# Products of a weight piece reordered: part, k tile, output tile in place of output tile, k tile, part

## The chip, the core and the metric

The kernel runs on one NeuronCore of a Trainium2 chip. TensorE (PE) multiplies, VectorE (DVE) and ScalarE (ACT) do everything elementwise, GpSimd (POOL) and SyncE (SP) issue transfers. The metric is the device time of one execution in microseconds, median of the runs.

## What is computed

Two layers of a decoder trunk for a prompt of 256 tokens and a sample group of 8 x 4 tokens, with shared weights. Layer 0 mixes tokens by causal pooling, layer 1 by multi-scale retention. The reference, cut to what matters here:

```python
for i in range(DEPTH):
    h = _rmsnorm(x, norm_mix[i])
    y = pool_mixer(h) if i % 2 == 0 else retention(h, ret_w_in, ret_w_out)
    x = x + y
    h = _rmsnorm(x, norm_ffn[i])
    u = einsum('btd,df->btf', h, w_up)          # 2048 -> 11264
    c = causal_conv3(u); gate, up = split(c)
    x = x + einsum('btf,fd->btd', silu(gate) * up, w_down)   # 5632 -> 2048
    gate = sigmoid(einsum('btd,de->bte', _rmsnorm(x, norm_ple[i]), ple_w_gate[i]))
    x = x + gate * einsum('btp,pd->btd', p[i], ple_w_proj[i])
return _rmsnorm(x, norm_final), new states
```

All in float32. D_MODEL is 2048, FFN_DIM 5632, PLE_DIM 256, 8 heads.

## The kernel before

Tokens lie on the free axis: 256 of the prompt and 32 of the sample make one moving operand of 288 columns. Weights are the stationary operand, 128 x 128 at a time. A float32 product is made of three products of the type fp32r: both the weights and the activations are split into a high and a low part, and hi·hi, hi·lo and lo·hi are added up in PSUM (the function `three`, lines 265 to 267; in the trace `xh,hi`, `xl,hi`, `xh,lo`, activations first).

The weights come in **pieces** of 256 x 512: two k tiles (`kk`) of 128 rows, four output tiles (`m`) of 128 columns. A piece is loaded into `raw`, ScalarE casts it to `hi` (L1402), VectorE subtracts to get `lo` (L1410). A piece takes 24 products: 4 output tiles x 2 k tiles x 3 parts. There are 864 pieces, and 20,736 such products.

Pieces belong to **groups**: one group makes four output tiles and runs over all its K rows, `K // 2` pieces. The 168 groups are, in order: pooling (4 groups of 2 pieces), per FFN 22 up groups of 8 pieces and 24 down groups of 2 or 4, per embedding 4 gate groups of 8 pieces and 4 groups `emb` of one piece, and in the retention 8 groups each for q and k (A), v (B) and the gate (C), of 8 pieces, and 32 output groups (O) of 2.

Each output tile of a group adds up in a PSUM bank of its own, taken from a ring of five (`pbank`, name `mm`). When the last piece of a group is through with output tile m, `g.evac` is issued at once: it reads the bank on VectorE (lines 604 and 605 for an up group, 722 for down, 1361 for O, 1001 for C, 859 for emb, 532 for pooling) or ScalarE (958 for A, 993 with 994 on VectorE for B). The bank is free for the next group when that is done. A group needs four banks and the ring has five, so its first tile gets the bank that was left over, and tiles 1, 2 and 3 get those of tiles 0, 1 and 2 of the group before.

What is issued around the products is set by a program at build time: after each of the four quarters of a piece (6 products, a "tick") it issues operations of other work on the engines' queues, by estimated clocks. The cast of the piece after next is issued at the start of a piece, and its subtraction after the third quarter's products, ahead of the eviction of tile 2:

```python
            split_hi(i + AHEAD)
            ...
                if m == 2:
                    split_lo(i + AHEAD)
                if last:
                    g.evac(m, ps)
```

Of the kernel before, what the change touches and what calls it, by code (L numbers as in the profile page):

```python
# [21 lines left out]
NT = NP + NS  # L22
FFN = 5632
# [82 lines left out]
def trunk_kernel(ctx: ExitStack, tc: tile.TileContext, I: dict, O: dict):  # L106
# [31 lines left out]

    # ---------------------------------------------------------------- scheduling
    # The product stream is emitted tile by tile; between two tiles ("tick") single operations of  # L140
    # other work are emitted, when an estimate of the engines' clocks says that their inputs are
    # there and that the engine has time.
    main = deque()
# [100 lines left out]

    # ---------------------------------------------------------------- small helpers
    def rsqrt(y, v, t):
# [25 lines left out]

    # ---------------------------------------------------------------- norm of the next phase
    def ssq_ops(M):
# [54 lines left out]
    def finalize(M, ph):  # L329
        """x tile M is done: its square sum and its parts for the next products."""  # L330
        a, b = ssq_ops(M), xg_ops(M, ph)
        main.extend([a[0], b[0]])
        main.extend(lag)
        lag[:] = [b[1]] + a[1:]
        if M == 15:
            main.extend(lag)
            last = tuple(lag)
            lag.clear()
            main.extend(norm_ops(ph, last))
# [19 lines left out]

    # ---------------------------------------------------------------- layer 0 mixer: pooling  # L360
    class PoolPhase:
# [36 lines left out]
        def start(self):  # L398
            V.memset(ones, 1.0)
            V.memset(ssq, 1.0)  # L400
            for i in range(4):
                if i == 3:
                    A.activation(self.sqs[:, 0:512], self.x4, AF.Square, accum_out=tiny[:, 8:9])
                t = (self.x0, self.x1)[i // 2][:, (i % 2) * (D // 2):(i % 2 + 1) * (D // 2)]
                A.activation(self.sqs[:, 0:D // 2], t, AF.Square, accum_out=tiny[:, 9 + i:10 + i])
            for q in range(4):
                self.xT(0, q, True)
            self.xT(1, 0, False)
            self.xT(1, 1, False)
            px = pbank()  # L410
            for j in range(4):
                to_tr(px[:, 128 * j:128 * j + 128], self.x4[:, 128 * j:128 * j + 128], 128)
            ps = sbank()
            T.matmul(ps[:32, 0:1], self.pc[:, 5], tiny[:, 8:9], start=True, stop=True)
            self.xT(1, 2, False)
            self.xT(1, 3, False)
            pp = sbank()
            to_tr(pp[:, 0:128], self.prow, 128)
            # products of no use, that the tensor engine's clock stays up while the norm is worked out
            pw = sbank()  # L420
            for _ in range(8):
                T.matmul(pw[:, 0:128], ones, ones, start=True, stop=True)
            release(pw)
            V.tensor_tensor(ssq[:, 0:1], tiny[:, 9:10], tiny[:, 10:11], ADD)
            V.tensor_copy(ssq[:32, 2:3], ps[:32, 0:1])
            release(ps)
            V.tensor_tensor(ssq[:, 1:2], tiny[:, 11:12], tiny[:, 12:13], ADD)
            rms_r()
            A.copy(x[:, :, 256:288].rearrange("p (c j) t -> p c j t", j=4),
                   px.rearrange("p (j c t) -> p c j t", j=4, c=4))  # L430
            A.copy(par, pp[:, 0:128])
            release(pp)
            clk["P"] = clk["A"] = clk["V"] = 13500.0
            V.tensor_scalar(self.pc[:32, 0:4], self.pc[:32, 0:4], rtok[:32, 2:3], None, MUL)
            self.direct(self.weigh(0))
            chains = self.quad(0)
            self.direct(self.sbg(0))
            w = self.weigh(1) + self.sbg(1)
            ops = skew(chains + self.quad(1))
            for n, op in enumerate(ops):  # L440
                self.direct([op])
                if n == 5:
                    self.direct(w)
                if n in (9, 15):
                    split_hi(n // 10)
                if n in (12, 18):
                    split_lo(n // 13)
# [95 lines left out]

    # ---------------------------------------------------------------- conv FFN
    class FfnPhase:
# [191 lines left out]

    # ---------------------------------------------------------------- per layer embedding
    class PlePhase:
# [36 lines left out]
        def build(self):  # L776
            l, nxt = self.l, self.nxt
# [25 lines left out]
            def finish():  # L803
                """the last four tiles: their squares go to the sums one by one"""
                flush()
# [94 lines left out]

    # ---------------------------------------------------------------- layer 1 mixer: retention
    class RetPhase:
# [50 lines left out]

        # -- q, k of a head are there
        def qk_evac(self, m, ps, h):
# [52 lines left out]

        # -- everything per head besides the projections, in stages, one per slot
        def attention(self, h):  # L1010
# [13 lines left out]

            # the sample's parts of q and k
            def loads():
# [25 lines left out]

            # prompt scores
            def scores():
# [47 lines left out]

            # the sample's scores and its k, four times on the partitions: (kh, kh, kl, kl)
            def stacks():
# [19 lines left out]

            # v on the tokens, the sample's as (vh, vl, vh, vl)
            def vr_():
# [47 lines left out]

            # the prompt's output and its last state
            on = [None] * 3
# [32 lines left out]

            # the sample's states, half by half  # L1210
            def sh_(b, kk):
# [37 lines left out]
            def half(i):  # L1249
                """hi of half i; lo of it is to follow"""  # L1250
                b, kk = divmod(i, 2)
                op = loaded[b] if kk == 0 else oa(512, lambda: sh_(b, 1))
                add(f"sh{i}", op, f"out{i - 3}" if i >= 3 else "")
# [122 lines left out]

    # ---------------------------------------------------------------- program
    pool = PoolPhase()
# [36 lines left out]
    with tc.manual_schedule():  # L1415
        pool.loads()
        pool.start()
        for i, (g, j) in enumerate(pieces):
# [9 lines left out]
            for m in range(4):  # L1428
                if j == 0:
                    g.ps[m] = pbank()  # L1430
                ps = g.ps[m]
                c = slice(128 * m, 128 * m + 128)
                for kk in range(2):
                    mh, ml = g.mov(2 * j + kk)
                    s = j == 0 and kk == 0
                    three(ps[:, :NT], (h[:, kk, c], l[:, kk, c]), (mh, ml), s, last and kk == 1)
                charge("P", TICK)
                if m == 2:
                    split_lo(i + AHEAD)
                if last:  # L1440
                    g.evac(m, ps)
                    charge(g.eng, 400, clk["P"] + LAT)
# [36 lines left out]
```

## Time and profile before

| what | value |
|---|---|
| runs: median of 3 (lowest, highest) | 3023.69 us (3023.5, 3026.85) |
| span of the profiled execution, first to last instruction | 3020.6 us |
| PE busy, products and other matmuls | 2998.1 us (99%), 22,019 |
| DVE busy | 1963.7 us (65%) |
| ACT busy | 1416.2 us (47%) |
| mean granted TensorE clock | 0.995 of full speed |

The span is the time of the one profiled execution from its first to its last instruction; the median of the runs is 3.1 us above it. Matmuls are recorded as overlapping (a 288-column product lasts some 0.29 us and the next starts 0.13 us later), so the steps between starts tell more than the busy time. A bracket at the end of a row of the timeline is the engine's idle time before it and who ended it.

### The profile page before, as it was taken

The page shows a single profiled execution, that of the slowest core. Times are in us where ns is not written, and L with a number is a line of the kernel's source. Part 1 is how long each engine was busy: PE and PEld are TensorE (multiplying, and loading weights), DVE is VectorE, ACT ScalarE, POOL GpSimd, SP SyncE. Part 2 cuts the span into 40 slices and gives each one's busy share as a digit, 9 for nine tenths or more (in the row PEclk, how much of TensorE's full clock was granted, in tenths as well). Part 3 has the DMA queues.
Part 4 walks back from the last instruction along what each step waited for, and adds up shares of the span by engine and source line. Part 5 has one row for each costly group of instructions (what it writes and reads, how often), then busy time and mean ns, then how long its engine had stood idle before and what let it go on. Part 6 is the DMA issues. An engine that isn't in the chain of part 4 may idle for free.

```text
span 3020.6 us, 54260 instructions
## 1 busy us (share of the span) xinstructions
PE 2998.1 (99%) x22019; PEld 2945.6 (98%) x22019; DVE 1963.7 (65%) x3396; ACT 1416.2 (47%) x2144; POOL 96.0 (3%) x131
## 2 busy tenths in 40 slices
PE   8999999999999999999999999999999999999998
PEld 8999999999999999999999999999999999999998
DVE  6666756565656767766766767676666565656565
ACT  4544434343444555445444444455444343434454
POOL 3000000000000000000000000000000000000000
PEclk8999999999999999999999999999999999999999
DMA  5655555555555566765766657566555555555543
GB/s 173 176 167 163 165 168 161 168 164 167 166 174 163 167 201 218 238 209 180 237 196 219 221 176 233 191 199 182 163 167 162 167 165 167 164 168 161 178 158 116
DMA packets 287906, 541.81 MB, mean 179 GB/s; under 512 B 18553, under 2 KB 55001, under 8 KB 287465
## 3 DMA queue, kind: packets, MB, share of 16 engines
q1 hardware_dynamic: 274968, 495.44, 53.5%
q0 software_dynamic: 12688, 42.91, 4.2%
q8 instruction: 173, 2.83, 0.4%
q14 instruction: 77, 0.63, 0.1%
HBM read 496.15 MB, written 42.84 MB: 178 GB/s over the span
## 4 chain that ended last, share of the span: by engine, by line
PE 98%; DVE 0%; DMA 0%; ACT 0%; issue 0%; SPq 0%; ACTq 0%
PE mm L265 31%; PE mm L267 30%; PE mm L266 30%; PE ms L262 1%; PE ms L1241 1%; PE ms L1225 1%; PE ms L1242 1%; PE ms L266 0%; PE ms L267 0%; PE ms L265 0%; DMA x<-in_x_prompt 0%; PE ms L1057 0%; PE ms L487 0%; PE ms L491 0%; PE ms L488 0%
## 5 line engine op out<-in xcount | busy, mean ns | idle before, releaser
L1402 ACT CAST hi<-raw 128x1024 fp32r<-128x1024 f32 x864 | 907.1, 1050 | 1393.0 <-PE mm L266 1185.1
L265 PE MATMUL mm<-xh,hi 128*128 128x288 f32 x4928 | 1465.2, 297 | 0.1
L266 PE MATMUL mm<-xl,hi 128*128 128x288 f32 x4928 | 1454.5, 295 | 0.0
L267 PE MATMUL mm<-xh,lo 128*128 128x288 f32 x4928 | 1449.7, 294 | 0.0
L1410 DVE TENSOR_TENSOR lo<-raw,hi 128x1024 fp32r<-128x1024 f32 x864 | 1054.4, 1221 | 552.0 <-ACT hi L1402 550.3
L265 PEld LDWEIGHTS mm<-xh,hi 128*128 128x128 f32 x4928 | 924.5, 188 | 12.1 <-DVE x L532 0.3
L266 PEld LDWEIGHTS mm<-xl,hi 128*128 128x128 f32 x4928 | 925.9, 188 | 4.7
L267 PEld LDWEIGHTS mm<-xh,lo 128*128 128x128 f32 x4928 | 928.4, 188 | 0.0
L266 PE MATMUL mm<-hl,hi 128*128 128x288 f32 x1408 | 415.4, 295 | 0.0
L267 PE MATMUL mm<-hh,lo 128*128 128x288 f32 x1408 | 415.1, 295 | 0.0
L265 PE MATMUL mm<-hh,hi 128*128 128x288 f32 x1408 | 413.3, 294 | 0.0
L265 PEld LDWEIGHTS mm<-hh,hi 128*128 128x128 f32 x1408 | 264.7, 188 | 0.0
L266 PEld LDWEIGHTS mm<-hl,hi 128*128 128x128 f32 x1408 | 264.7, 188 | 0.0
L267 PEld LDWEIGHTS mm<-hh,lo 128*128 128x128 f32 x1408 | 264.5, 188 | 0.0
L632 DVE SCALAR_TENSOR_TENSOR c<-U,cv,c 128x304 f32<-128x304 f32 x352 | 179.4, 529 | 3.5 <-ACT c L629 0.4
L265 PE MATMUL mm<-rhh,hi 128*128 128x288 f32 x512 | 152.2, 297 | 0.0
L267 PE MATMUL mm<-rhh,lo 128*128 128x288 f32 x512 | 151.5, 296 | 0.0
L266 PE MATMUL mm<-rhl,hi 128*128 128x288 f32 x512 | 149.8, 293 | 0.4 <-DVE rhl L1319 0.4
L722 DVE TENSOR_TENSOR x<-x,mm 128x288 f32<-128x288 f32 x192 | 82.5, 450 | 86.5 <-PE mm L267 86.5
L604 DVE TENSOR_TENSOR U<-mm,rb 128x256 f32<-128x256 f32 x176 | 73.7, 419 | 94.8 <-PE mm L267 94.8
L629 ACT ACTIVATE c<-U,cv 128x304 f32<-128x304 f32 x176 | 107.6, 635 | 15.4 <-DVE U L605 15.4
L1229 DVE SCALAR_TENSOR_TENSOR S<-S,ms 128x512 f32<-128x512 f32 x128 | 87.0, 681 | 37.0 <-PE ms L1225 36.8
(265 smaller groups left out, 2154.9 us busy)
## 6 DMA issues: line engine op xcount, KB each, us to landing
raw<-in_ffn_w_up SPq DMA_DIRECT2D x352, 512.0 KB
raw<-in_ffn_w_down SPq DMA_DIRECT2D x176, 512.0 KB
raw<-in_ret_w_in SPq DMA_DIRECT2D x128, 512.0 KB
raw<-in_ple_w_gate SPq DMA_DIRECT2D x64, 512.0 KB
raw<-in_ret_w_in SPq DMA_DIRECT2D x128, 256.0 KB
S<-in_state_ret SPq DMA_DIRECT2D x64, 512.0 KB
out_ret_s<-S POOLq DMA_DIRECT2D x64, 512.0 KB, 4.2
raw<-in_ret_w_out SPq DMA_DIRECT2D x64, 512.0 KB
```

The lines of the kernel that those rows point to most:

```text
L262: T.transpose(out, in_, ident[:rows, :rows])
L265: T.matmul(out, w[0], a[0], start=start, stop=False)
L266: T.matmul(out, w[0], a[1], start=False, stop=False)
L267: T.matmul(out, w[1], a[0], start=False, stop=stop)
L604: V.tensor_tensor(U[:, s, 2:258], ps[:, 0:256], rb[:, 0:256], MUL)
L629: A.activation(c[0][:, 0:304], u[:, 2:306], AF.Identity, bias=w(3), scale=w(2))
L632: V.scalar_tensor_tensor(c[0][:, 0:304], u[:, s:304 + s], w(s), c[0][:, 0:304], MUL, ADD)
L722: V.tensor_tensor(x[:, M], x[:, M], ps[:, :NT], ADD)
L1225: T.matmul(ps, st["km", b][:, 128 * kk:128 * kk + 128], self.vst, start=True, stop=True)
L1229: V.scalar_tensor_tensor(s[:, kk], s[:, kk], g ** 4, st["u", b, kk], MUL, ADD)
L1402: A.copy(h, raw[i])
L1410: V.tensor_tensor(l, r, h.bitcast(F32), SUB)
```

## The change

Inside a piece that is not the last of its group, the 24 products are issued in another order. Before, output tile by output tile: for each m, both k tiles, and for each of these the three parts; six products in a row add onto one bank. After, part by part: the eight hi·hi products, then the eight with the low part of the activations, then the eight with the low part of the weights; inside a part k tile by k tile, and inside that the four output tiles, so that each product adds onto another bank than the one before. A tick still follows every six products. The last piece of a group (all of an `emb` group) keeps the old order. In the first piece of a group the four banks are taken at its first four products.

```diff
             for m in range(4):
-                if j == 0:
-                    g.ps[m] = pbank()
-                ps = g.ps[m]
-                c = slice(128 * m, 128 * m + 128)
-                for kk in range(2):
-                    mh, ml = g.mov(2 * j + kk)
-                    s = j == 0 and kk == 0
-                    three(ps[:, :NT], (h[:, kk, c], l[:, kk, c]), (mh, ml), s, last and kk == 1)
+                if last:
+                    if j == 0:
+                        g.ps[m] = pbank()
+                    ps = g.ps[m]
+                    c = slice(128 * m, 128 * m + 128)
+                    for kk in range(2):
+                        mh, ml = g.mov(2 * j + kk)
+                        s = j == 0 and kk == 0
+                        three(ps[:, :NT], (h[:, kk, c], l[:, kk, c]), (mh, ml), s, last and kk == 1)
+                else:
+                    for n in range(6 * m, 6 * m + 6):
+                        part, kk, mt = n // 8, (n // 4) % 2, n % 4
+                        if j == 0 and n < 4:
+                            g.ps[mt] = pbank()
+                        w = (l if part == 2 else h)[:, kk, 128 * mt:128 * mt + 128]
+                        a = g.mov(2 * j + kk)[part == 1]
+                        T.matmul(g.ps[mt][:, :NT], w, a, start=j == 0 and n < 4, stop=False)
                 charge("P", TICK)
                 if m == 2:
                     split_lo(i + AHEAD)
                 if last:
-                    g.evac(m, ps)
+                    g.evac(m, g.ps[m])
```

On TensorE, at the end of the first and the start of the second up group of layer 0, the order before is this; `mm_...` are the banks' buffers, `hi_...` and `lo_...` the piece's parts, `xh` and `xl` the activations', and the brackets name the engines that an instruction waits for:

```order
L265 MATMUL mm_1079<-xh_74,hi_1222 128x288
L266 MATMUL mm_1079<-xl_75,hi_1222 128x288
L267 MATMUL mm_1079<-xh_74,lo_1244 128x288
L265 MATMUL mm_1327<-xh_74,hi_1252 128x288 [waits Activation_49]
L266 MATMUL mm_1327<-xl_75,hi_1252 128x288
L267 MATMUL mm_1327<-xh_74,lo_1274 128x288 [waits DVE_49]
L265 MATMUL mm_1327<-xh_74,hi_1252 128x288
L266 MATMUL mm_1327<-xl_75,hi_1252 128x288
L267 MATMUL mm_1327<-xh_74,lo_1274 128x288
L265 MATMUL mm_1335<-xh_74,hi_1252 128x288 [waits DVE_49,PE_49]
L266 MATMUL mm_1335<-xl_75,hi_1252 128x288
L267 MATMUL mm_1335<-xh_74,lo_1274 128x288
```

The second, third and fourth bank are asked for at the 7th, 13th and 19th product. At the same place after the change:

```order
L265 MATMUL mm_1058<-xh_74,hi_1222 128x288
L266 MATMUL mm_1058<-xl_75,hi_1222 128x288
L267 MATMUL mm_1058<-xh_74,lo_1244 128x288
L1446 MATMUL mm_1327<-xh_74,hi_1252 128x288 [waits Activation_49]
L1446 MATMUL mm_1329<-xh_74,hi_1252 128x288 [waits DVE_49,PE_49]
L1446 MATMUL mm_1331<-xh_74,hi_1252 128x288 [waits DVE_49,PE_49]
L1446 MATMUL mm_1333<-xh_74,hi_1252 128x288 [waits DVE_49,PE_49]
L1446 MATMUL mm_1327<-xh_74,hi_1252 128x288
L1446 MATMUL mm_1329<-xh_74,hi_1252 128x288
L1446 MATMUL mm_1331<-xh_74,hi_1252 128x288
L1446 MATMUL mm_1333<-xh_74,hi_1252 128x288
L1446 MATMUL mm_1327<-xl_75,hi_1252 128x288
```

The three waits for evicted banks now stand at the 2nd, 3rd and 4th product, and the low part of the weights is first used by the 17th product, where it was the 3rd.

VectorE's order does not change. At the end of an up group of layer 0 it is, before:

```order
L604 TENSOR_TENSOR U_681<-mm_2757,rb_76 128x256 [waits PE_49]
L605 TENSOR_TENSOR U_681<-mm_2757,rb_76 128x8x4
L604 TENSOR_TENSOR U_681<-mm_2766,rb_76 128x256 [waits PE_49]
L605 TENSOR_TENSOR U_681<-mm_2766,rb_76 128x8x4
L1410 TENSOR_TENSOR lo_3003<-raw_2889,hi_2977 128x1024 [waits DMAHW5_49,Activation_49]
L604 TENSOR_TENSOR U_681<-mm_2776,rb_76 128x256 [waits PE_49]
L605 TENSOR_TENSOR U_681<-mm_2776,rb_76 128x8x4
L604 TENSOR_TENSOR U_681<-mm_2785,rb_76 128x256 [waits PE_49]
```

and after:

```order
L604 TENSOR_TENSOR U_681<-mm_2757,rb_76 128x256 [waits PE_49]
L605 TENSOR_TENSOR U_681<-mm_2757,rb_76 128x8x4
L604 TENSOR_TENSOR U_681<-mm_2759,rb_76 128x256 [waits PE_49]
L605 TENSOR_TENSOR U_681<-mm_2759,rb_76 128x8x4
L1410 TENSOR_TENSOR lo_3003<-raw_2889,hi_2977 128x1024 [waits DMAHW5_49,Activation_49]
L604 TENSOR_TENSOR U_681<-mm_2761,rb_76 128x256 [waits PE_49]
L605 TENSOR_TENSOR U_681<-mm_2761,rb_76 128x8x4
L604 TENSOR_TENSOR U_681<-mm_2763,rb_76 128x256 [waits PE_49]
```

The evictions of tiles 0 and 1, the subtraction of a later piece, and the evictions of tiles 2 and 3 follow each other as before; only the numbers of the buffers differ.

## Rows read from the trace of the kernel before

**Rows 1.** The page's head and the busy time of each engine

```profile
span 3020.6 us, 54260 instructions
PE 2998.1 (99%) x22019; PEld 2945.6 (98%) x22019; DVE 1963.7 (65%) x3396; ACT 1416.2 (47%) x2144; POOL 96.0 (3%) x131
```

**Rows 2.** Waits of TensorE: who waited for whom, us, times, longest

```profile
PE mm L266 <- DVE rhl L1319: 0.4, 1, 0.4
```

**Rows 3.** Stretches: busy us of PE, PEld, DVE, ACT, POOL; clock, DMA share, GB/s

```profile
2200.00:2600.00 400.00, 400.00 (x3010) 400.00 (x3009) 245.27 (x410) 174.46 (x245) 0.00 (x0) 1.00 0.56 166
69.00:72.00 3.00, 2.93 (x23) 2.69 (x22) 3.00 (x7) 0.95 (x4) 0.38 (x1) 1.00 0.92 343
38.30:40.50 2.20, 2.20 (x11) 2.20 (x10) 1.88 (x5) 1.63 (x4) 0.00 (x0) 0.50 0.61 229
```

**Rows 4.** TensorE's timeline, start and length in us, at two ends of an output tile

```profile
61.52 0.30 PE L267 MATMUL mm<-xh,lo 128*128 128x288 f32 x1
61.66 0.29 PE L265 MATMUL mm<-xh,hi 128*128 128x288 f32 x1
...
3003.67 0.29 PE L267 MATMUL mm<-ph,lo 128*128 128x288 f32 x1
3003.80 0.30 PE L265 MATMUL mm<-ph,hi 128*128 128x288 f32 x1
```

**Rows 5.** TensorE's timeline: the first product of an up group

```profile
639.24 0.29 PE L265 MATMUL mm<-xh,hi 128*128 128x288 f32 x1
```

**Rows 6.** VectorE's timeline around that product

```profile
638.18 0.18 DVE L605 TENSOR_TENSOR U<-mm,rb 128x32 f32<-128x32 f32 x1
638.28 1.22 DVE L1410 TENSOR_TENSOR lo<-raw,hi 128x1024 fp32r<-128x1024 f32 x1
639.41 0.42 DVE L604 TENSOR_TENSOR U<-mm,rb 128x256 f32<-128x256 f32 x1
639.74 0.18 DVE L605 TENSOR_TENSOR U<-mm,rb 128x32 f32<-128x32 f32 x1
```

**Rows 7.** TensorE's timeline in the third and fourth pooling group

```profile
67.25 0.29 PE L265 MATMUL mm<-xh,hi 128*128 128x288 f32 x1
...
69.52 0.29 PE L267 MATMUL mm<-xh,lo 128*128 128x288 f32 x1
69.88 0.40 PE L265 MATMUL mm<-xh,hi 128*128 128x288 f32 x1
70.12 0.29 PE L266 MATMUL mm<-xl,hi 128*128 128x288 f32 x1
```

**Rows 8.** VectorE's timeline there: the eviction of a third pooling tile

```profile
69.32 0.51 DVE L532 SCALAR_TENSOR_TENSOR x<-mm,par,x 128x288 f32<-128x288 f32 x1
```

**Rows 9.** TensorE's timeline: a group's first product after down, emb0, emb1

```profile
371.20 0.29 PE L265 MATMUL mm<-hh,hi 128*128 128x288 f32 x1
...
952.48 0.29 PE L265 MATMUL mm<-xh,hi 128*128 128x288 f32 x1
...
2974.50 0.29 PE L265 MATMUL mm<-xh,hi 128*128 128x288 f32 x1
```

**Rows 10.** VectorE's timeline: the eviction of tile 2 at the same three places

```profile
371.32 0.45 DVE L722 TENSOR_TENSOR x<-x,mm 128x288 f32<-128x288 f32 x1
...
952.81 0.45 DVE L859 TENSOR_TENSOR sg<-mm,sg 128x288 f32<-128x288 f32 x1
...
2975.24 0.45 DVE L859 TENSOR_TENSOR sg<-mm,sg 128x288 f32<-128x288 f32 x1
```

**Rows 11.** Groups of instructions by line: count, busy us, mean ns; idle before

```profile
L722 DVE TENSOR_TENSOR x<-x,mm 128x288 f32<-128x288 f32 x192 | 82.5, 450 | 86.5 <-PE mm L267 86.5
L604 DVE TENSOR_TENSOR U<-mm,rb 128x256 f32<-128x256 f32 x176 | 73.7, 419 | 94.8 <-PE mm L267 94.8
L1361 DVE TENSOR_TENSOR x<-x,mm 128x288 f32<-128x288 f32 x128 | 54.9, 450 | 67.2 <-PE mm L267 67.2
L859 DVE TENSOR_TENSOR sg<-mm,sg 128x288 f32<-128x288 f32 x32 | 14.1, 452 | 2.8 <-PE mm L267 1.8
L1001 DVE TENSOR_TENSOR rsg<-mm,rb 128x288 f32<-128x288 f32 x32 | 13.8, 452 | 9.1 <-PE mm L267 9.1
L958 ACT COPY fm<-mm 128x288 f32<-128x288 f32 x32 | 12.8, 401 | 8.5 <-PE mm L267 8.4
```

## The prediction, made before the changed kernel ran

> **What bounds the kernel now.** I read the page's head first: TensorE is busy for 99% of a span of 3020.6 us, VectorE for 65%, ScalarE for 47% [rows 1]. The list of waits then says whether TensorE is ever held up: after the first 60 us it names one wait, 0.4 us for a low part of the retention's output [rows 2]. A stretch from the middle shows what this means: 400 us, of which TensorE is busy 400, with 3010 products, so a step of 400 / 3010 = 132.9 ns at full clock [rows 3]. So the kernel is a row of 20,736 steps of 0.133 us, 2757 us in all, plus other matmuls. Two things can move its time: the length of a step, and a wait where there is none today. Whatever makes TensorE wait is paid in full, since nothing later on that engine has slack to give it back.
>
> **Does the step get shorter?** The change sends 696 of the 864 pieces (all but the 168 last ones) in an order in which each product adds onto another bank than its forerunner: 16,704 products. If adding twice in a row onto one bank held a product up, the step at the end of an output tile, where today's order goes to another bank, would be shorter than the five steps inside a tile. From 60 us on there are 3203 such steps with no other matmul between; the first goes from 61.52 to 61.66, the last from 3003.67 to 3003.80 [rows 4], and their mean is 132.9 ns. The steps inside a tile, position by position, have means from 132.8 to 133.3 once the few after other matmuls are left out, the overall mean again [rows 3]. So a change of bank neither gains nor costs, to within some 0.4 ns, which over 16,704 products is 7 us either way. I take 0. As bounds from further off: the same product at half the clock takes 2.20 us / 9 = 0.24 us (of the 11 products in that stretch two had started before it, [rows 3]); half of it, 0.12, is the least that a step at full clock could be, 217 us in all.
>
> The Trainium skill (Perfetto Trace Analysis, Matmul Optimizations) asks that all PSUM banks be used so that instructions can run side by side, and its page TensorE: Matmul & The Clock Gate (Back-to-back issue gap) gives columns / 2.4 + 2.5 ns for a step, an estimate of 122.5 ns here; by that the change could win up to 16,704 x 10.4 ns = 174 us. The trace disagrees with the figure, 132.9 ns, and the sum goes by the row.
>
> **The wait that it adds.** A group takes banks from a ring of five. Its tiles 1 to 3 get the banks of tiles 0 to 2 of the group before, and must wait until these are evicted. Today tile 3 asks for its bank at the 19th product, 18 x 0.133 = 2.4 us after the group's first. Now it asks at the 4th, 0.4 us after it. What is late is the eviction of tile 2, for on VectorE the subtraction that makes a later piece's `lo` stands ahead of it, 1.22 us long.
>
> An up group shows it [rows 5, 6]. Its first product starts at P = 639.24. VectorE ended the eviction of tile 1 of the group before at 638.18 + 0.18 = 638.36, in time for the third product at P + 0.27 by more than 1 us, and tile 0 still earlier. Then come the subtraction from 638.28 and both halves of the eviction of tile 2, which ends at E = 639.74 + 0.18 = 639.92. The fourth product is due at P + 0.40 = 639.64. Today nobody notices, since tile 3 asks at 641.6.
>
> What a late eviction costs is seen once in this trace, in the pooling stage: an eviction ends at 69.32 + 0.51 = 69.83 [rows 8], the waiting product starts at 69.88 where 69.65 was due, and the product after it at 70.12 [rows 7]. So the second product starts 0.29 us after E. Undisturbed, the fifth product of a group starts at P + 4 x 0.133 = P + 0.53. The loss is then E + 0.29 - (P + 0.53) = **(E - P) - 0.24 us**, for each group whose forerunner is evicted like this. VectorE's order stays, the evictions hang on the last piece, which keeps its old order, and VectorE waits for TensorE at the first two evictions of a group, so that it carries no backlog into them: E - P should stay what it is today.
>
> By kind of forerunner, counts from the evictions, four of each line per group [rows 11]:
>
> - up: 176 / 4 = 44 groups, E - P = 0.68, loss 0.44: 19.4 us [rows 5, 6].
> - down, O and C evict with the same kind of instruction, 450, 450 and 452 ns: 192 / 4 + 128 / 4 + 32 / 4 = 88 groups. After down E = 371.32 + 0.45 = 371.77 and P = 371.20, so 0.57 and a loss of 0.33 [rows 9, 10]: 29.0 us.
> - emb: in layer 0 E - P = 953.26 - 952.48 = 0.78, loss 0.54, four times: 2.2 us. In layer 1 another addition for each tile stands in the queue: 2975.69 - 2974.50 = 1.19, loss 0.95, three times (the fourth ends the kernel): 2.9 us [rows 9, 10].
> - pooling: the third group's forerunner is evicted so late that the fourth group would wait 69.83 - 67.25 - 0.24 = 2.34 us; today's order already loses (69.88 - 69.52) + (70.12 - 69.88) - 0.27 = 0.33 of it, so 2.0 more [rows 7, 8]. For the boundary into the FFN I add 0.4, like an up group; VectorE is behind there, and it could be anything up to 1 us.
> - B: ScalarE evicts the most of it, VectorE a short rest that also stands behind the subtraction. No row fits; between nothing and 0.33 I take the middle, 0.17 eight times: 1.4 us.
> - A: ScalarE alone (401 ns), and its long work, the cast, is issued at the start of a piece, ahead of all four evictions. Nothing; if it were as bad as the others, 2.6 us.
> - gate: its successor is a group of one piece, which keeps the old order. Nothing.
>
> Taken away is the 0.4 us wait of [rows 2], since the low parts are used 6 products or more later than today. The release of `hi` comes 8 products earlier, which lets ScalarE cast sooner; no engine on the path waits for that.
>
> Sum: 19.4 + 29.0 + 2.2 + 2.9 + 2.0 + 0.4 + 1.4 - 0.4 = 56.9 us. The profiled execution would go from 3020.6 to 3077.5 us; the median of the runs stands 3.1 us above its span, so **3081 us**, 1.9% slower.
>
> **The rivals.**
>
> *The step does get shorter* (the other side). If a product onto the same bank does wait, in a way that a single change of bank in six does not show because the queue behind it is full, steps could fall towards 0.12 us: 217 us less, 57 more, 2864 us. The kernel is faster from a gain of 57 / 16,704 = 3.4 ns per product on. Against it stand the 3203 steps; for it only that no run of alternating products of this shape is in the trace. Chance 0.05.
>
> *The clock falls.* If some 150 short stops made the gate take the clock to 1.2 GHz for a time, every product in it would take 0.24 instead of 0.133 us; in 5% of the span that is 1037 products, 111 us, and 3190 us in all. The pooling stop of 0.36 us speaks against it: the granted clock is 1.00 in the stretch around it [rows 3], and each stop here is shorter or little longer. The Trainium skill (TensorE: Matmul & The Clock Gate, A second HAM failure mode: psum-queue depth-cycling) reports a kernel that cycled its PSUM banks, idled briefly between groups, and had its clock go up and down; no row here shows that. With it I put a step that lengthens by more than 1 ns, 17 us or more. Together 0.06.
>
> *A smaller stop.* If the earlier cast let VectorE take the subtraction before the eviction of tile 1, tile 2's would come up to 0.4 us sooner, and most of the loss would go: 3024 to 3060 us. The queue's order, which is fixed, speaks against it. Chance 0.06.
>
> *The change doesn't do what it says*: the fourth bank is not one that was just in use, and nothing waits; 3024 us. The order of the ring speaks against it. Chance 0.02.
>
> **How the numbers follow.** My forecast gets the remaining 0.81. Its unknowns are the restart after a wait, known from one stop only (0.05 us more or less on 150 stops is 7 us), the step (7 us), and the kinds without a row (1.4 down, 2.6 up): together, not all at once, 3064 to 3098. That holds 0.8 of the chance, so I don't widen it. A measurement of this kernel tells about 0.2% (6 us) from no change. Faster by more: 0.05; within: 0.02; slower by more: 0.93.
>
> **What would show it.** Right: TensorE's list of waits names the evictions on VectorE (lines 604/605, 722, 1361, 1001, 859) as what L1446 waited for, once per group, near 0.4 us after up and 0.3 after down; the middle of a group keeps 0.133 us per product; the granted clock stays at 1.00; the subtraction still stands ahead of the late eviction. Wrong: steps in L1446 other than 0.133, a wait at the 2nd or 3rd product, waits for `hi` or `lo`, a lower clock in mid-span, or evictions of tile 2 that move relative to the group's end.

## The result, and the profile after

The changed kernel takes 3073.41 us (median of 4 runs, 3072.2 to 3078.0), the kernel before 3023.67: a ratio of 1.0165, 95% interval 1.0152 to 1.0177. It is slower by 50 us, inside the stated range and 8 us below the forecast of 3081. The profiled execution is the longest of the four runs (3078.0 us, a span of 3076.2; forecast for it: 3077.5).

The page of the changed kernel: its head, the busy time, and the chain of work that ended last by engine and by line.

```profile
span 3076.2 us, 54253 instructions
PE 3028.4 (98%) x22019; PEld 2943.2 (96%) x22019; DVE 1964.4 (64%) x3396; ACT 1420.5 (46%) x2144; POOL 96.1 (3%) x131
...
PE 84%; DVE 9%; issue 5%; DMA 1%; ACT 0%; POOL 0%; DVEq 0%; ACTq 0%; POOLq 0%; SPq 0%
PE mm L1446 69%; DVE lo L1410 6%; PE mm L267 3%; PE mm L265 3%; PE mm L266 3%; PE ms L262 1%; PE ms L1242 1%; PE ms L1241 1%; PE ms L1225 1%; DVE x L722 1%; DVE U L604 1%; DMA x<-in_x_prompt 0%; DVE x L1361 0%; DVE U L605 0%; PE ms L267 0%
```

The work is the same (compare [rows 1]). In the kernel before, the chain lay on TensorE almost alone:

```profile
PE 98%; DVE 0%; DMA 0%; ACT 0%; issue 0%; SPq 0%; ACTq 0%
```

Now it crosses VectorE: the subtraction L1410, 6% of the span, and the evictions behind it. A line in the chain says that something waited for it; 6% is the time that the chain spends there, not what it costs.

The list of waits of TensorE (us in total, times, longest), only its rows for the products in the new order:

```profile
PE mm L1446 <- DVE U L605: 11.9, 44, 0.3
...
PE mm L1446 <- DVE sg L859: 3.1, 7, 0.7
...
PE mm L1446 <- DVE x L532: 2.3, 2, 2.1
...
PE mm L1446 <- DVE x L1361: 0.5, 1, 0.5
```

All are evictions, but the list holds 17.8 us of a loss of 50, and down (L722) is missing. That is a trap of this view: a product is recorded 0.29 us long where the step is 0.133, so the first 0.16 us of a stop are covered by the record of the product before, and of a stop behind down only 0.06 us are left, which the list leaves out. The view of line 1446, which counts weight loads too (engine idle before it, us, times), has them all:

```profile
  issue: 21.1, 44
  DVE x L722: 14.4, 48
  DVE U L605: 11.9, 44
  DVE x L1361: 10.2, 32
  DVE sg L859: 7.9, 14
  DVE x L532: 5.0, 4
  DVE rsg L1001: 2.3, 8
  DVE vsf L994: 1.3, 8
```

These are the counts of the prediction: 44 up groups, 48 down, 32 O, 8 C, 8 B. The 44 under "issue" are the weight loads of the products that wait behind an up group (one of them below, at 653.50). The sums are not to be added up, since weight load and product are idle side by side.

A boundary between two up groups, on TensorE and then on VectorE (start, length, us), the one that answers to [rows 5, 6]:

```profile
652.70 0.56 PE L1446 MATMUL mm<-xh,hi 128*128 128x288 f32 x3
653.53 0.91 PE L1446 MATMUL mm<-xh,hi 128*128 128x288 f32 x5 [0.27 <-DVE U L605]
654.27 0.29 PE L1446 MATMUL mm<-xl,hi 128*128 128x288 f32 x1
```

```profile
651.73 1.22 DVE L1410 TENSOR_TENSOR lo<-raw,hi 128x1024 fp32r<-128x1024 f32 x1
652.87 0.42 DVE L604 TENSOR_TENSOR U<-mm,rb 128x256 f32<-128x256 f32 x1
653.20 0.18 DVE L605 TENSOR_TENSOR U<-mm,rb 128x32 f32<-128x32 f32 x1
```

Three products go, the fourth waits. P = 652.70 and E = 653.20 + 0.18 = 653.38, so E - P = 0.68, as predicted. The ninth product, due at P + 8 x 0.133 = 653.76, starts at 654.27: the stop costs 0.51 us.

From the starts of all products I added up what the first five steps of the 159 groups concerned take beyond 133 ns each (the first of these groups starts at 49 us, the last at 3030). It is 61.2 us after and 0.8 before. By the kind of group that comes before:

| forerunner | groups | predicted, us | measured, us | measured per group |
|---|---|---|---|---|
| up | 44 | 19.4 | 22.5 | 0.51 |
| down, O, C | 88 | 29.0 | 29.2 | 0.33 |
| emb of layer 0 / layer 1 | 4 / 3 | 2.2 / 2.9 | 2.2 / 2.9 | 0.54 / 0.95 |
| pooling | 4 | 2.4, and 0.3 paid before | 3.0 | |
| B | 8 | 1.4 | 1.5 | 0.19 |
| A | 8 | 0 | 0.0 | 0 |

Against these 60 us more stand steps that are shorter than predicted. Means of all steps after 60 us with no other matmul between and none above 145 ns: 132.99 ns before, 132.5 in the changed kernel's new order (some 16,000 steps). Compared step by step with the kernel before, the steps of the new order give back 9.7 us.

The spans of the two traces differ by 55.6 us. Beside the 60.4 of the waits and the -9.7 of the steps, 3.0 us are 32 products at half the clock (told further down), 3.1 us stand beside other matmuls, nearly all at 1076 and 1178 us, where the list of waits has three rows that the kernel before hasn't, and -1.2 us are what is left at the start, at the end and in the last pieces.

```profile
PE ms L315 <- DVE acc L310: 1.3, 1, 1.3
...
PE ms L1241 <- ACT Sh L1213: 0.5, 1, 0.5
...
PE ms L1242 <- DVE Sl L1217: 0.3, 1, 0.3
```

That the change made these three is not shown: line 315 and its like wait at this place, for 1.3 to 2.1 us, in the profiles of three kernels below that have no waits on evictions (tile, part, k tile; the diagonal; parts mixed).

### The profile page after: what moved, and what is told of

The parts are those of the page before. It is cut to its first block, busy times and chain, and to the rows that moved or that the text cites. A ratio compares the mean times of both kernels' runs of the same rounds, so it can differ in the third digit from the quotient of the medians.

```text
span 3076.2 us, 54253 instructions
## 1 busy us (share of the span) xinstructions
PE 3028.4 (98%) x22019; PEld 2943.2 (96%) x22019; DVE 1964.4 (64%) x3396; ACT 1420.5 (46%) x2144; POOL 96.1 (3%) x131
## 4 chain that ended last, share of the span: by engine, by line
PE 84%; DVE 9%; issue 5%; DMA 1%; ACT 0%; POOL 0%; DVEq 0%; ACTq 0%; POOLq 0%; SPq 0%
PE mm L1446 69%; DVE lo L1410 6%; PE mm L267 3%; PE mm L265 3%; PE mm L266 3%; PE ms L262 1%; PE ms L1242 1%; PE ms L1241 1%; PE ms L1225 1%; DVE x L722 1%; DVE U L604 1%; DMA x<-in_x_prompt 0%; DVE x L1361 0%; DVE U L605 0%; PE ms L267 0%
## 5 line engine op out<-in xcount | busy, mean ns | idle before, releaser
L1410 DVE TENSOR_TENSOR lo<-raw,hi 128x1024 fp32r<-128x1024 f32 x864 | 1054.8, 1221 | 504.0 <-ACT hi L1402 502.1
L1446 PE MATMUL mm<-xh,hi 128*128 128x288 f32 x4288 | 687.5, 298 | 16.1 <-DVE U L605 9.2
L1446 PE MATMUL mm<-xl,hi 128*128 128x288 f32 x4288 | 670.8, 296 | 0.0
L1446 PE MATMUL mm<-xh,lo 128*128 128x288 f32 x4288 | 661.2, 296 | 0.0
L1446 PEld LDWEIGHTS mm<-xh,hi 128*128 128x128 f32 x4288 | 607.7, 188 | 38.8 <-issue 16.3
L1446 PEld LDWEIGHTS mm<-xl,hi 128*128 128x128 f32 x4288 | 604.8, 188 | 7.4
L1446 PEld LDWEIGHTS mm<-xh,lo 128*128 128x128 f32 x4288 | 600.0, 189 | 0.1
L267 PE MATMUL mm<-xh,lo 128*128 128x288 f32 x640 | 189.2, 296 | 0.0
L266 PE MATMUL mm<-xl,hi 128*128 128x288 f32 x640 | 189.2, 296 | 0.0
L265 PE MATMUL mm<-xh,hi 128*128 128x288 f32 x640 | 189.0, 295 | 0.0
L1446 PE MATMUL mm<-hh,hi 128*128 128x288 f32 x1024 | 169.2, 300 | 5.2 <-DVE U L605 2.7
L1446 PEld LDWEIGHTS mm<-hh,hi 128*128 128x128 f32 x1024 | 144.4, 188 | 16.2 <-DVE x L722 11.4
L722 DVE TENSOR_TENSOR x<-x,mm 128x288 f32<-128x288 f32 x192 | 82.7, 452 | 121.0 <-PE mm L267 121.0
L1446 PE MATMUL mm<-hh,lo 128*128 128x288 f32 x1024 | 156.9, 295 | 0.0
L1446 PE MATMUL mm<-hl,hi 128*128 128x288 f32 x1024 | 156.2, 295 | 0.0
L1446 PEld LDWEIGHTS mm<-hh,lo 128*128 128x128 f32 x1024 | 143.0, 188 | 0.0
L1446 PEld LDWEIGHTS mm<-hl,hi 128*128 128x128 f32 x1024 | 142.6, 188 | 0.0
L265 PEld LDWEIGHTS mm<-xh,hi 128*128 128x128 f32 x640 | 120.5, 188 | 0.8
```

The costliest lines, as they stand in the source:

```text
L265: T.matmul(out, w[0], a[0], start=start, stop=False)
L266: T.matmul(out, w[0], a[1], start=False, stop=False)
L267: T.matmul(out, w[1], a[0], start=False, stop=stop)
L722: V.tensor_tensor(x[:, M], x[:, M], ps[:, :NT], ADD)
L1410: V.tensor_tensor(l, r, h.bitcast(F32), SUB)
L1446: T.matmul(g.ps[mt][:, :NT], w, a, start=j == 0 and n < 4, stop=False)
```

## The experiments

Each was timed in five rounds beside the kernel before. Times are medians; the ratio is to the kernel before, with its 95% interval. Theory 1: the loss is the wait for tile 2's bank. Theory 2, its rival: the order costs by itself.

**The subtraction behind the eviction.** The changed kernel with this edit in the loop:

```diff
-                if m == 2:
+                if m == 2 and not last:
                     split_lo(i + AHEAD)
                 if last:
                     g.evac(m, g.ps[m])
+                    if m == 2:
+                        split_lo(i + AHEAD)
```

> The changed kernel, with the subtraction of the later piece issued behind the eviction of tile 2 in a group's last piece, not ahead of it. If the whole loss is the wait for tile 2's bank (theory 1), the waits in L1446 for evictions go (some 60 us of them in the profile), and what is left is the step, 0.6 ns shorter per product in the profile of the changed kernel (16,400 steps, 10 us): about 3014 us, and in no case above 3024. If the new order costs by itself, by its changes of bank at every product (theory 2), it stays near 3073 us.

Measured: 3013.91 us, ratio 0.9964 (0.9952 to 0.9977). No wait in L1446 is left in the list, and the product order is the changed kernel's. Behind an up group the eviction of tile 2 now ends 0.08 us before the next group's first product, where it ended 0.68 us after it, and the first five steps of the 159 groups take 0.1 us too long in place of 61.2. Theory 1 holds, theory 2 falls: with the wait gone the new order is faster than the old.

**The same edit in the kernel before**, with `g.evac(m, ps)`:

> The kernel before, with the subtraction issued behind the eviction of tile 2 in a group's last piece: the control of e1_evict_first. In the old order tile 2's bank is asked for 2.4 us into the group, so theory 1 says 3024 us, within 3 us. If the place of the subtraction is worth something by itself, it shows here.

Measured: 3024.41 us, ratio 0.9999 (0.9991 to 1.0008). The edit is worth nothing where nobody asks early.

**Only the first piece in the old order**, and **only the first piece in the new**. Two kernels, each the changed one with one line edited:

```diff
-                if last:
+                if last or j == 0:
```

```diff
-                if last:
+                if last or j > 0:
```

> The changed kernel, but the first piece of each group keeps the old order too: 536 pieces in the new order, and no early demand for banks. Theory 1 (the wait): no waits on evictions, and 12,864 products at a step shorter by 0.6 ns: 3016 us, between 3013 and 3024. Theory 2 (the order itself costs): 536/696 of 50 us, so about 3062 us.

> The kernel before, with only the first piece of each group in the new order (160 pieces). Theory 1: all of the waits, 61 us, and 3,840 steps shorter by 0.6 ns: 3082 us, slower than the changed kernel. Theory 2: 160/696 of 50 us, about 3035 us.

Measured: 3015.36 us, ratio 0.9973 (0.9961 to 0.9984), and 3081.8 us, ratio 1.019 (1.0177 to 1.0204). The 160 first pieces carry the whole loss, and more: with them alone in the new order the kernel is slower than with all 696. Its list of waits repeats that of the changed kernel:

```profile
PE mm L1446 <- DVE U L605: 12.0, 44, 0.3
...
PE mm L1446 <- DVE sg L859: 3.2, 7, 0.7
...
PE mm L1446 <- DVE x L532: 2.3, 2, 2.1
PE mm L1446 <- DVE x L1361: 0.5, 1, 0.5
```

So the wait was settled, and the shorter step was what I had not expected. The next runs take the evictions-first kernel and change only the order of the 24 products; the edit that puts evictions first, and in the two tile-by-tile versions the lines by which a tile's bank is taken at its own first product, are left out of the cuts. Theory A: it is the change of bank. B: products in a row with the same moving operand. C: the parts grouped.

Tile, part, k tile: one bank for six products, no moving operand twice in a row.

```diff
-                    for n in range(6 * m, 6 * m + 6):
-                        part, kk, mt = n // 8, (n // 4) % 2, n % 4
+                    for n in range(6):
+                        part, kk, mt = n // 2, n % 2, m
```

> As e1_evict_first, but the middle loops are output tile, part, k tile: six products in a row on one bank again, each with another moving operand than the one before. If the step of 132.45 ns in the new order comes from the changes of bank (theory A), it is 133.0 ns here and the time 3024 us. If it comes from four products in a row with the same moving operand (theory B), 133.0 ns and 3024 us as well. If grouping the parts does it (theory C), 132.45 ns and 3014 us.

Measured: 3025.67 us, ratio 1.0 (0.9991 to 1.0008). Theory C falls.

A diagonal: the bank and nearly always the moving operand change.

```diff
-                        part, kk, mt = n // 8, (n // 4) % 2, n % 4
+                        mt, s = n % 4, (n // 4 + n % 4) % 6
+                        part, kk = s // 2, s % 2
```

> As e1_evict_first, but on a diagonal: each product on another bank than the one before, and with another moving operand than the one before but for a few. Theory A (banks): a step of 132.45 ns, 3014 us. Theory B (same moving operand): 133.0 ns, 3024 us. Theory C (parts grouped): 133.0 ns, 3024 us.

Measured: 3010.47 us, ratio 0.9948 (0.9936 to 0.9961). Theory B falls. A is not the whole either: the step is 131.9 ns where the evictions-first kernel has 132.4. The two times alone, 3010 and 3014 us, have overlapping intervals.

Tile by tile with a third of the moving operands kept:

```diff
-                    for n in range(6 * m, 6 * m + 6):
-                        part, kk, mt = n // 8, (n // 4) % 2, n % 4
+                    for n in range(6):
+                        part, kk, mt = (1, 0, 2)[n % 3], n // 3, m
```

> As e1_evict_first, but tile by tile as before the change, with the three parts in the order hi weights x low activations, hi x hi, low weights x hi: one step in three has the moving operand of the one before, and five of six stay on the bank. Theory A: 133.0 ns, 3024 us. Theory B: a third of the steps where the new order has three quarters, so 132.75 ns and 3020 us. Theory C: 133.0 ns, 3024 us.

Measured: 3026.54 us, ratio 1.0004 (0.9995 to 1.0013). On one bank the moving operand makes no difference.

Another bank at each product, and the moving operand kept as often as can be:

```diff
-                        part, kk, mt = n // 8, (n // 4) % 2, n % 4
+                        kk, part, mt = n // 12, (0, 2, 1)[(n // 4) % 3], n % 4
```

> As e1_evict_first, with the loops k tile, part, output tile and the parts in the order hi x hi, low weights x hi, hi weights x low: another bank at every product, and seven of twelve and three of twelve products in a row with the same moving operand (10 of 12 steps, where the new order has 9 of 12). Theory A: 132.45 ns, 3014 us. Theory B: 132.4 ns, 3013 us. Theory C: parts are grouped less, 133.0 ns and 3024 us.

Measured: 3016.78 us, ratio 0.9972 (0.9961 to 0.9983), near what A and B had; C falls again. (In that expectation seven and three are the steps; the products in a row are eight and four.)

Then the diagonal was taken apart: the moving operand changing with the parts grouped, and the parts mixed with the moving operand kept.

```diff
-                        part, kk, mt = n // 8, (n // 4) % 2, n % 4
+                        part, mt = n // 8, n % 4
+                        kk = (n // 4 + mt) % 2
```

```diff
-                        part, kk, mt = n // 8, (n // 4) % 2, n % 4
+                        mt, s = n % 4, (n // 4 + n % 4 // 2) % 6
+                        part, kk = s // 2, s % 2
```

> As e1_evict_first, part by part as the change has it, but the k tile alternates from product to product: 3 of the 23 steps inside a piece keep the moving operand, where the change keeps it in 18. In e6_diagonal (2 of 23) the step was 131.89 ns, in e1_evict_first 132.43, in e8 (20 of 23) 132.52. Theory M (a bank change gives 0.5 ns, and a change of moving operand on top of it another 0.5): 131.9 ns, 3010 us. Theory P (what e6 has over e1 comes from mixing the parts, so that weights come from two tiles in turn): 132.45 ns, 3014 us.

> As e6_diagonal, parts mixed and another bank at each product, but with the shift for every second output tile only: 17 of the 23 steps keep the moving operand. Theory M: 132.4 ns, 3014 us. Theory P: 131.9 ns, 3010 us.

Measured: 3006.63 us, ratio 0.9934 (0.9921 to 0.9946), the fastest version here, and 3017.68 us, ratio 0.9972 (0.9961 to 0.9982). The steps are 131.9 and 132.5 ns: theory M holds in both, P in neither. But where the moving operand changes from product to product, here and in the diagonal, the k tile alternates, and the rows of the weights alternate with it; no run changes the one without the other.

Last, how many banks it takes. The changed kernel with its subtraction where it was, the tiles in pairs:

```diff
-                        part, kk, mt = n // 8, (n // 4) % 2, n % 4
-                        if j == 0 and n < 4:
+                        mt, s = 2 * (n // 12) + n % 2, (n % 12 // 2 + 3 * (n % 2)) % 6
+                        part, kk = s // 2, s % 2
+                        if j == 0 and n % 12 < 2:
                             g.ps[mt] = pbank()
...
-                        T.matmul(g.ps[mt][:, :NT], w, a, start=j == 0 and n < 4, stop=False)
+                        T.matmul(g.ps[mt][:, :NT], w, a, start=j == 0 and n % 12 < 2, stop=False)
```

> The changed kernel, subtraction where the change leaves it (ahead of the eviction of tile 2), but output tiles in pairs: twelve products in turn on the banks of tiles 0 and 1, then twelve on those of 2 and 3, the moving operand kept in 4 of 23 steps. The bank of tile 3 is asked for by the 14th product, 1.7 us into the group, when its eviction ended 0.6 to 1.2 us into it: by theory 1 no waits. If two banks in turn are enough for the shorter step, and a change of moving operand adds to it (theory M): 131.9 ns and 3007 us. If it takes more than two banks: 133.0 ns and 3024 us. If the loss of the changed kernel comes of alternating banks and not of the early demand: above 3060 us.

Measured: 3040.61 us, ratio 1.0047 (1.0033 to 1.006). The waits at the starts of the groups are gone, 0.6 us in place of 61, though the subtraction still stands ahead of the eviction: theory 1 once more, by the demand alone. The step is longer than with one bank, 133.2 ns by the mean of those up to 145 ns, which no theory had; most of the 17 us come from some 650 steps above 145 ns, where the other orders have some 100. So its mix of operands was run on four banks, from the diagonal:

```diff
-                        mt, s = n % 4, (n // 4 + n % 4) % 6
+                        mt, s = n % 4, (n // 4 + 3 * (n % 2)) % 6
```

> As e6_diagonal (four banks in turn, evictions first), but with the mix of operands of e11_two_banks: the odd products are three steps of the list of part and k tile ahead of the even ones, and few keep the moving operand. e11 had a step of 133.2 ns and no waits on evictions. If a bank needs three products between two additions on it (theory D, distance), the step is 131.9 ns here and the time 3008 us. If the mix of operands made e11 slow (theory O), the step stays at 133.2 ns and the time near 3035 us.

Measured: 3009.59 us, ratio 0.9946 (0.9932 to 0.9959): theory D, the mix is not to blame. Three banks in turn were not tried.

The steps side by side. One stretch in five of the kernels; the columns are those of [rows 3], and 400 us over the count of products gives the step, 0.1 ns short of the means of starts, since two of the products counted began before the stretch. First the kernel with the subtraction behind the eviction (132.4 ns), where [rows 3] have 132.9:

```profile
2200.00:2600.00 400.00, 400.00 (x3022) 400.00 (x3021) 247.76 (x412) 181.40 (x252) 0.00 (x0) 1.00 0.56 166
```

the one with alternating k tiles (131.9 ns):

```profile
2200.00:2600.00 400.00, 400.00 (x3032) 400.00 (x3031) 248.53 (x412) 181.54 (x252) 0.00 (x0) 1.00 0.53 167
```

the tile-by-tile one with pairs of the same moving operand (132.9 ns):

```profile
2200.00:2600.00 400.00, 400.00 (x3010) 400.00 (x3009) 249.51 (x417) 175.97 (x245) 0.00 (x0) 1.00 0.52 166
```

the one with two banks in turn (133.6 ns):

```profile
2200.00:2600.00 400.00, 400.00 (x2993) 400.00 (x2992) 245.63 (x412) 174.58 (x242) 0.00 (x0) 1.00 0.52 164
```

and the one with the same mix on four (131.9 ns):

```profile
2200.00:2600.00 400.00, 400.00 (x3032) 400.00 (x3031) 248.74 (x413) 179.01 (x253) 0.00 (x0) 1.00 0.53 167
```

## Why the prediction was right, and where a term was off

**The wait.** Right in place, kind and size. The formula (E - P) - 0.24 us, taken from one stop in the trace of before, gave 29.0 us for down, O and C where 29.2 were measured, and the emb, B and A terms to within 0.1 us. E - P did not move, as argued from VectorE's order. The runs show the cause: put the subtraction behind the eviction, or ask for the banks later (first piece old, two banks), and the stops go; ask early in the old kernel, and they come.

**Up groups, mis-sized.** Predicted 0.44, measured 0.51 us each, 3 us in all. E - P was as predicted; the restart took longer. Behind down, an eviction of tile 2 ends at 549.04 + 0.45 = 549.49, and the weight load that waits for it and its product start together, 0.05 to 0.06 us later. Behind the up group above (E = 653.38), the load starts 0.12 us after the eviction and the product, at 653.53, 0.15 us after it. An eviction and a weight load behind down, then the weight load behind up:

```profile
549.04 0.45 DVE L722 TENSOR_TENSOR x<-x,mm 128x288 f32<-128x288 f32 x1
...
549.55 0.30 PEld L1446 LDWEIGHTS mm<-hh,hi 128*128 128x128 f32 x2 [0.30 <-DVE x L722]
...
653.50 0.18 PEld L1446 LDWEIGHTS mm<-xh,hi 128*128 128x128 f32 x1 [0.48 <-issue]
```

The order of before and after shows two waits on that product, for VectorE and for TensorE's own earlier products. The view of line 1446 has 166 separate semaphore instructions of 51 ns; one stands among the first products behind each of the 44 up groups, and none behind any other kind. That these 51 ns are most of what the restart pays fits, but was not tried by itself.

**The step, mis-sized.** "I take 0" was wrong by 0.5 to 0.6 ns, 9.7 us, just past the 0.4 ns given as its bound. The step that failed is the inference from the changes of bank at the end of a tile: a single change in six shows 0.1 ns, a change at every product over four banks 0.5 to 1.1. That is the side of the first rival, at a sixth of the 3.4 ns that would have decided. Its mechanism, that a product waits when it adds onto the bank of the one before, is not shown: with two banks in turn no product inside a piece does so, and the step is longer, not shorter.

The Trainium skill (Perfetto Trace Analysis, Matmul Optimizations), with its advice to use all the banks, pointed the right way for four banks. The formula of its page TensorE: Matmul & The Clock Gate (Back-to-back issue gap), which the section gives for a matmul by itself and the prediction took for a stream, would leave 10.4 ns to gain; the runs show 1.1 at best.

**The sum.** The wait was +60.4 for a forecast of +57, the step -9.7 for 0. That the profiled span still grew by 55.6 us for a forecast of 56.9 is in part luck: the half clock and the waits beside other matmuls, 6.1 us that no term had, made up for most of the step. The median lies 8 us below the forecast mostly because the profiled run was 4.6 us above the median of its kernel, where I had taken the distance of before.

**The rivals.** No smaller stop and no missing wait. In the middle of the kernel the clock stayed at 1.00 through the stops of 0.3 to 0.5 us: the stretch from 2200 to 2600 us, in which 23 such groups begin, shows it:

```profile
2200.00:2600.00 400.00, 396.26 (x2949) 391.16 (x2948) 240.36 (x402) 171.31 (x237) 0.00 (x0) 1.00 0.54 162
```

But the prediction's argument, that each stop is shorter than 0.36 us or little longer, left out its own pooling stop of 2.34 us, and behind that one the clock did fall, from full (2.4 GHz) to half (1.2). Two stretches of the changed kernel, 66 to 69 us with the stop, listed as 2.1 us, and 72 to 75 us behind it (busy PE, PEld, DVE, ACT, POOL; then the granted clock):

```profile
66.00:69.00 3.00, 1.42 (x11) 1.18 (x9) 1.92 (x4) 2.70 (x4) 1.23 (x2) 1.00 0.97 285
...
72.00:75.00 3.00, 3.00 (x17) 3.00 (x16) 0.32 (x2) 0.89 (x1) 3.00 (x6) 0.59 0.78 256
```

17 products are recorded there, two of which began before; at full clock 15 take 2.0 us, so some 1.0 us are lost in these 3 us. A second dip stands at 1078 to 1081 us, in the retention's start, behind the wait of line 315, and it is one of the prediction's signs of being wrong. Both together cost 3.0 us. That the waits on evictions brought them on is not shown, and two runs speak against it. The kernel with only the first pieces in the new order has the same stop at the same place, 2.1 us, and full clock behind it; and that with the last mix on four banks, which has no such stop, falls to half at 63 us, with TensorE busy throughout the 9 us before. First the one, then the other:

```profile
72.00:75.00 3.00, 3.00 (x24) 3.00 (x24) 1.56 (x3) 1.12 (x2) 3.00 (x6) 1.00 0.71 251
...
63.00:66.00 3.00, 3.00 (x14) 2.96 (x14) 2.36 (x5) 2.26 (x5) 2.78 (x1) 0.54 0.00 0
```

Five more kernels without waits on evictions dip at 60 to 63 us. What decides it is open. The kernel with alternating k tiles goes through four banks in turn and holds 1.00 from 44 to 2992 us. The dips that the Trainium skill tells of (TensorE: Matmul & The Clock Gate, A second HAM failure mode: psum-queue depth-cycling) did not follow there from the cycling of banks.

## What to carry to other kernels

When an order is changed so that several accumulators are opened at once, look at when each bank is asked for, and against that at the end of its last eviction with all that stands ahead of it in that engine's queue; a few hundred nanoseconds per group were 2% here, and one line in the other engine's order took them away. In a kernel in which one engine is always busy, a stop can be priced from a single earlier stop in the trace, and the price held for 88 groups to 1% in sum; behind the 44 up groups, where the restart was another, it was 0.07 us short. A list of waits hides stops that are shorter than the recorded overlap of the matmuls; count starts instead.

## What was not expected of the hardware

The step of a 288-column fp32r product at full clock depends on the order by up to 1.1 ns, by the means of the steps up to 145 ns: 133.0 ns (132.9 to 133.1) on one bank for six products, whether the moving operand changes or not; 132.4 to 132.5 over four banks in turn with the moving operand kept in 17 to 20 of 23 steps; 131.9 over four banks with it changing in 20 or 21; and 133.2, with more irregular steps that bring it to 133.6 in mid-span, over two banks in turn. The three kernels at 131.9 (diagonal, alternating k tiles, four banks with the last mix) agree though their parts are ordered differently. That the order over four banks shortens the step is shown. That it is the moving operand that makes the last 0.5 ns is not: in all three the k tile alternates between products, for weights and activations alike. What in the engine or the memories makes it so stays open, as does why two banks are worse than one.

At half the clock (1.2 GHz) the same product took 0.24 us a step [rows 3], half of which is 0.12; at full clock the step is 0.133. What holds it back there is also open.
